# A new order of projections, a scheduler that prices dependent steps, and a second staging tile for values

## The chip, the cores and the metric

The kernel runs on one core of a Trainium2 chip. The metric is device time in microseconds; lower is better. The time before is a median of three runs, 1429.63 us (1425.99 to 1433.2).

## The reference, cut to what matters

One layer over 2048 frames of width 1024, with three groups of heads side by side, all in float32:

```python
u = x @ w_in
(fq, fk, fv, ff, fz, mq, mk, mv, mi, mf, mo, mz, rq, rz) = jnp.split(u, split_points, axis=-1)
y_fox = forgetting_attention(fq, fk, fv, ff + fox_f_bias) * jax.nn.silu(fz)
qk = jax.nn.silu(causal_depthwise_conv(jnp.concatenate([mq, mk], axis=-1), conv_w, conv_b))
mq_c, mk_c = jnp.split(qk, [MLSTM_WIDTH], axis=-1)
y_ml = mlstm(mq_c, mk_c, mv, mi + i_bias, mf + f_bias, mo, norm_g) * jax.nn.silu(mz)
mem_k, mem_v = jnp.split(mem @ w_mem_kv, [MEM_WIDTH], axis=-1)
y_mem = memory_attention(rq, mem_k, mem_v) * jax.nn.silu(rz)
y = jnp.concatenate([y_fox, y_ml, y_mem], axis=-1) @ w_out
return layer_norm(DEEPNORM_ALPHA * x + y, ln_g, ln_b)
```

`forgetting_attention` is causal softmax attention with 6 heads of 64, whose logits carry `c[query] - c[key]`, with `c` the running sum of the log forget gates. `mlstm` is a recurrent matrix memory with 4 heads of 96, computed in chunks; each chunk needs the state that the chunk before left. `memory_attention` is softmax attention of 4 heads of 64 into 256 memory tokens. A convolution over four frames and a SiLU stand before the mLSTM's queries and keys.

## The kernel before, in words

Every float32 operand of a large product is split into a high and a low part, and a product is three matmuls (high x high, low x high, high x low). The sequence is cut into four blocks of 512 frames, in two halves (`hf` 0 and 1, `bi` 0 and 1 within a half).

The kernel's work is written as small threads (Python generators). Each yields the next engine operation or asks for tiles. `Machine` (from line 131) is a list scheduler that runs while the program is built: it keeps a clock for each engine, gives each operation a price (`Op`, lines 91 to 112) and a time at which its inputs are there (`Machine.when`), and issues the ready operation with the lowest priority number on the engine that can start first. The times are a model's. What it fixes is the order of instructions on each engine; on the chip each engine takes its instructions in that order and waits where an input or a buffer isn't there.

- Projections (`projections`, one thread) run in the order of the list `SEQ`, one string for each half. An entry is a kind and a number, for both blocks or, with `.0` or `.1`, for one: `gate` (the gate logits and the attention's values), `mk mk mv` (memory keys and values), `rq` (memory queries, two heads each), `h` (queries and keys of one attention head), `y` and `z` (SiLU gates), `r` (the mLSTM's rows: values, output gate, gate), `c` (the mLSTM's queries and keys; each block gets a convolution of three multiply-add taps on VectorE, tile `cv`). One entry for one block is 24 matmuls of 512 columns, or 4 x 24 of 384 or 398 for `r` and `gate`. They go to PSUM tiles `pj`.
- Weights come by a loader: a DMA into `raw`, the high part `h` by ScalarE, the low part `l` by VectorE. High and low of a piece take one tile each of the tag `w`, together.
- In a `gate` job each of four row tiles is followed by `post`: the gate logits are added to `g14`, the values are split into high and low in a staging tile `vs` (ScalarE, then VectorE), and a DMA writes it to the scratch tensor `v_all`. When all eight tiles of a half are through, `gates` runs: log-sigmoid steps on VectorE up to the tiles `lsp`, which TensorE transposes, then cumulative sums (`tensor_tensor_scan`) on VectorE.
- Attention is a queue of 40 items (one head, one block; 0 to 7 and 20 to 27 are memory attention). For each, `att_max` (scores with queries in rows, tile `mx`, maxima on VectorE), `att_qk` and `att_exp` (scores `st`, two exponentials on ScalarE into `ph` and `p`, the low part `pl` on VectorE, the sum of `p` into `acc` on GpSimd) and `att_pv` (product `o` with the values) work in chunks of 128 keys; items run one after another in each. Items 32 to 35 are heads 2 and 3 of the second half, 36 to 39 heads 4 and 5. An item of block 2 has 12 chunks, one of block 3 has 16.
- The 16 mLSTM units (`ml_unit`, 128 frames each) start when all weights of the projections have been asked for and the last attention item is queued. Units are chains of short steps on all engines, and tile by tile they depend on the state.
- The output stage (`out_tile`) does the last product, for 16 tiles of 128 frames, once the mLSTM and all attention of a block are there.

`BUFS` gives the number of buffers of each tag; a thread that finds none waits.

Of the kernel before, what the change touches and what calls it, by code (L numbers as in the profile page):

```python
# [73 lines left out]
class Op:  # L74


    def __init__(self, eng, fn, args, kw):
# [8 lines left out]
        cols = size(out)  # L86
# [4 lines left out]
        if eng == "PE":  # L91
            f32 = ins[0].dtype == F32
            if f32 and fn.__name__ != "transpose":
                self.cost = 2.0 * max(2.0 * cols / 2.4, 107.0)
            else:
                self.cost = max((2.0 if f32 else 1.0) * cols / 2.4 + 14.0, 110.0)
        elif eng == "ACT":
            self.cost = 70.0 + 0.835 * wide + 115.0 * sum(hasattr(kw.get(a), "tensor") for a in ("bias", "scale"))
        elif eng == "DVE":
            one = fn.__name__ in ("tensor_scalar", "tensor_copy")  # L100
            columns = sum(size(a) == 1 for a in ins)
            self.cost = 69.0 + (0.521 if one else 1.042) * wide + 60.0 * columns
        elif eng == "POOL":
            if kw.get("op") == ALU.pow:
                self.cost = 290.0 + 170.0 * cols
            else:
                self.cost = 120.0 + (2.15 if fn.__name__ == "tensor_tensor" else 0.95) * wide
        else:
            self.cost = 475.0
            self.nbytes = 4 * math.prod(out.shape)  # L110
            self.far = 800.0 if kw["in_"].tensor.space == "DRAM" else 0.0
# [13 lines left out]
        self.key = (prio, seq)  # L125


LAT = 200.0
DMA_NS, DMA_BPNS = (600.0, 750.0), 366.0


class Machine:
# [54 lines left out]
    def when(self, op):  # L187
        eng, w = op.eng, 0.0
        for nm in op.ins + [op.out]:
            t, by = self.wr.get(nm, (0.0, eng))  # L190
            if by != eng or eng == "SP":
                w = max(w, t + LAT)
        return max(w, self.rd.get(op.out, 0.0))

    def issue(self, op):
# [70 lines left out]
class Engine:  # L266
# [5 lines left out]
    def __getattr__(self, fn):  # L272
# [1 line left out]
        return lambda *args, **kw: Op(self.name, f, args, kw)  # L274


BUFS = dict(x=32, raw=2, w=19, kb=6, qb=4, v=9, p=2, ph=2, pl=3, acc=1, zs=4, tz=2, vs=1, y=2, ta=4, sm=11, sc=2,
            rr=2, gs=4, g14=1, lsp=2, st=2, mx=2, pj=3, o=1)
PSUM_TAGS = ("st", "mx", "pj", "o")
RAW = ("raw", "p")  # L280
# [5 lines left out]
FAST = 8  # L286
LEAD = (1, 2)

SEQ = ("gate0 mk0.0 mk1.0 mv2.0 rq0 r0 y0 rq1 h0 y1 h1 r1 z0 h2 h3 r2 z1 c0 h4 c2 h5 c1 z2 c3.0 c4.0 c5.0 c3.1 c4.1 c5.1",
       "gate0 rq1 y1 rq0 y0 h0 r0 h1 z0 h2 r1 h3 z1 h4 c1 c2 c0.0 h5 z2 c0.1 r2 c4 c3.0 c5.1 c5.0 c3.1")  # L290


def _order():
# [1119 lines left out]
```

## Time and profile before

| what | value |
|---|---|
| median of the three runs | 1429.63 us |
| the profiled execution | 1436.65 us, span 1434.9 us |
| mean granted TensorE clock | 0.971 |
| TensorE busy (matmuls) | 1337.3 us, 93% |
| VectorE busy | 1057.1 us, 74% |
| ScalarE busy | 651.1 us, 45% |
| GpSimd busy | 486.5 us, 34% |
| DMA, mean over the span | 117 GB/s |

All instructions come from one helper, so all carry line 209, and groups are told apart by the names of their tiles: `out<-in`. PE is TensorE, DVE VectorE, ACT ScalarE, POOL GpSimd. A row of a window gives its ends, its length, the busy us of PE, PE's weight loads, DVE, ACT and POOL with their counts, the clock granted to TensorE, the busy share of the DMA engines and GB/s. A row of waits gives the total, the number of waits and the longest.

### The profile page before, as it was taken

The numbers are of one execution on the slowest core, as the hardware profiler recorded it, in microseconds if no ns is written. First come the engines' busy times: TensorE is split into PE (matmuls) and PEld (weight loads), VectorE is DVE, ScalarE is ACT, GpSimd is POOL, SyncE is SP. The second block draws the span as 40 slices with busy tenths as digits, with TensorE's granted clock in tenths as the row PEclk, the third lists the DMA queues.
The fourth block names the chain that finished last, engine by engine and source line by source line (L and its number), as shares of the span: only waits on it lengthen the run. The fifth ranks groups of instructions, "written<-read, shape, count | busy, mean of one in ns | idle before, by whom it ended". The sixth has DMA issues, their size and how long they took to land.

```text
span 1434.9 us, 20374 instructions
## 1 busy us (share of the span) xinstructions
PE 1337.3 (93%) x6648; PEld 1116.6 (78%) x6648; DVE 1057.1 (74%) x2082; ACT 651.1 (45%) x1371; POOL 486.5 (34%) x430
## 2 busy tenths in 40 slices
PE   7799999999999999899999998988999859999998
PEld 7778778888877897678887876656887648778886
DVE  4684687567578866879788878977888887668455
ACT  4423454335344542354536455453536676465100
POOL 3001233305103300025626456362544544355300
PEclk9999999999999999999999999999999969999999
DMA  6612421440531354141330431104012479775552
GB/s 205 224 46 78 136 74 62 128 127 23 171 110 54 114 177 144 51 142 57 100 97 18 135 107 49 50 30 126 33 44 92 128 211 281 218 211 176 195 164 85
DMA packets 136666, 167.54 MB, mean 117 GB/s; under 512 B 13760, under 2 KB 90832, under 8 KB 136560
## 3 DMA queue, kind: packets, MB, share of 16 engines
q1 hardware_dynamic: 136560, 166.24, 37.6%
q8 instruction: 53, 0.87, 0.3%
q14 instruction: 53, 0.43, 0.1%
HBM read 107.05 MB, written 50.29 MB: 110 GB/s over the span
## 4 chain that ended last, share of the span: by engine, by line
PE 62%; DVE 16%; DMA 9%; ACT 5%; issue 4%; POOL 3%; SPq 1%; DVEq 0%; ACTq 0%; POOLq 0%
PE pj L209 45%; PE st L209 6%; PE o L209 6%; PE mx L209 5%; DVE pl L209 3%; DMA v_all<-vs 3%; POOL acc L209 2%; DVE cv L209 2%; DMA dd<-m_scr 2%; DVE l L209 2%; DMA raw<-in_wg_dram 1%; DVE mp L209 1%; DVE mx L209 1%; DVE r L209 1%; ACT h L209 1%
## 5 line engine op out<-in xcount | busy, mean ns | idle before, releaser
L209 POOL TENSOR_TENSOR acc<-acc,p 128x512 f32<-128x512 f32 (+2 forms) x232 | 319.9, 1379 | 468.6 <-ACT p L209 174.1
L209 PE MATMUL pj<-h,h 128*128 128x512 f32 (+3 forms) x1144 | 428.0, 374 | 13.7 <-ACT h L209 8.8
L209 PE MATMUL pj<-l,h 128*128 128x512 f32 (+3 forms) x1144 | 421.1, 368 | 0.3 <-DVE l L209 0.2
L209 PE MATMUL pj<-h,l 128*128 128x512 f32 (+3 forms) x1144 | 421.0, 368 | 0.3
L209 PEld LDWEIGHTS pj<-h,h 128*128 128x128 f32 x1144 | 218.5, 191 | 41.0 <-ACT h L209 9.8
L209 PEld LDWEIGHTS pj<-l,h 128*128 128x128 f32 x1144 | 218.1, 191 | 27.8 <-DVE l L209 1.2
L209 PEld LDWEIGHTS pj<-h,l 128*128 128x128 f32 x1144 | 217.2, 190 | 27.5 <-DVE l L209 1.7
L209 DVE TENSOR_TENSOR pl<-p,ph 128x512 fp32r<-128x512 f32 (+2 forms) x185 | 190.8, 1038 | 29.6 <-ACT p L209 23.3
L209 ACT ACTIVATE ph<-st 128x512 fp32r<-128x512 f32 (+2 forms) x218 | 120.0, 555 | 101.1 <-PE st L209 88.4
L209 DVE TENSOR_TENSOR l<-raw,h 128x512 fp32r<-128x512 f32 (+2 forms) x194 | 137.7, 736 | 36.9 <-ACT h L209 35.4
L209 ACT ACTIVATE p<-st 128x512 f32<-128x512 f32 (+2 forms) x232 | 125.3, 546 | 46.6 <-POOL acc L209 27.3
L209 ACT CAST h<-raw 128x512 fp32r<-128x512 f32 (+2 forms) x194 | 108.3, 585 | 74.3 <-DMA raw<-in_wg_dram 40.8
L209 PE MATMUL o<-pl,v 128*128 128x512 f32 (+2 forms) x272 | 106.8, 396 | 13.6 <-DVE pl L209 13.1
L209 PE MATMUL st<-qm,km 68*128 68x512 f32 (+2 forms) x272 | 105.0, 386 | 11.5 <-ACT p L209 8.7
L209 PE MATMUL st<-qb,kb 128*128 128x512 f32 (+2 forms) x272 | 110.0, 404 | 0.0
L209 DVE TENSOR_REDUCE mp<-mx 128x1 f32<-128x512 f32 x144 | 95.3, 684 | 15.6 <-PE mx L209 14.7
L209 PE MATMUL pj<-h,yh 128*128 128x512 f32 (+1 forms) x264 | 106.2, 402 | 0.0
L209 PE MATMUL mx<-km,qm 66*128 66x512 f32 (+2 forms) x304 | 99.4, 366 | 7.2 <-DVE mp L209 2.8
L209 PE MATMUL pj<-h,ylo 128*128 128x512 f32 (+1 forms) x264 | 102.6, 389 | 0.0
L209 PE MATMUL pj<-l,yh 128*128 128x512 f32 (+1 forms) x264 | 102.1, 387 | 0.0
L209 PE MATMUL o<-ph,v 128*128 128x512 f32 (+2 forms) x218 | 84.0, 386 | 0.0
L209 POOL TENSOR_TENSOR y<-y,zs 128x512 f32<-128x512 f32 x20 | 30.2, 1512 | 146.4 <-DVE y L209 89.5
(184 smaller groups left out, 1929.4 us busy)
## 6 DMA issues: line engine op xcount, KB each, us to landing
raw<-in_wg_dram SPq DMA_DIRECT2D x76, 256.0 KB
raw<-in_wg_dram SPq DMA_DIRECT2D x48, 192.0 KB
v<-v_all SPq DMA_DIRECT2D x36, 256.0 KB
raw<-in_xt_dram SPq DMA_DIRECT2D x32, 256.0 KB
xr<-in_x_dram SPq DMA_DIRECT2D x32, 256.0 KB
out_dram<-xr SPq DMA_DIRECT2D x32, 256.0 KB
v_all<-vs SPq DMA_DIRECT2D x16, 384.0 KB
row_scr<-stg SPq DMA_DIRECT2D x32, 192.0 KB
```

Source lines behind the costliest of these rows:

```text
L209: op.fn(*op.args, **op.kw)
```

## The change

The scheduler's model: a scan on VectorE costs 60 + 2.3 ns a column (before, as any operation there, 69 + 1.042); the latency from one engine to another is taken as 300 ns (before 200); and an operation that reads what the same engine wrote waits 118 ns (not on TensorE). The smallest price of a four-pass float32 matmul goes from 107 to 112. Buffers: `vs` 1 to 2, `w` 19 to 18. `SEQ`: both strings are new. Each instruction does what it did; how many of each there are stays the same.

```diff
             if f32 and fn.__name__ != "transpose":
-                self.cost = 2.0 * max(2.0 * cols / 2.4, 107.0)
+                self.cost = 2.0 * max(2.0 * cols / 2.4, 112.0)
...
+        elif fn.__name__ == "tensor_tensor_scan":
+            self.cost = 60.0 + 2.3 * wide
         elif eng == "DVE":
...
-LAT = 200.0
+LAT, OWN = 300.0, 118.0
...
             if by != eng or eng == "SP":
                 w = max(w, t + LAT)
+            elif eng != "PE" and nm in op.ins:
+                w = max(w, t + OWN)
...
-BUFS = dict(x=32, raw=2, w=19, kb=6, qb=4, v=9, p=2, ph=2, pl=3, acc=1, zs=4, tz=2, vs=1, y=2, ta=4, sm=11, sc=2,
+BUFS = dict(x=32, raw=2, w=18, kb=6, qb=4, v=9, p=2, ph=2, pl=3, acc=1, zs=4, tz=2, vs=2, y=2, ta=4, sm=11, sc=2,
...
-SEQ = ("gate0 mk0.0 mk1.0 mv2.0 rq0 r0 y0 rq1 h0 y1 h1 r1 z0 h2 h3 r2 z1 c0 h4 c2 h5 c1 z2 c3.0 c4.0 c5.0 c3.1 c4.1 c5.1",
-       "gate0 rq1 y1 rq0 y0 h0 r0 h1 z0 h2 r1 h3 z1 h4 c1 c2 c0.0 h5 z2 c0.1 r2 c4 c3.0 c5.1 c5.0 c3.1")
+SEQ = ("gate0 mk0.0 mk1.0 mv2.0 rq0 r0 y0 y1 rq1 h0 h1 z0 r1 h2 c0 h3 z1 h4 h5 r2 c2 c3.0 z2 c1 c4.0 c5.0 c3.1 c4.1 c5.1",
+       "rq0 gate0 rq1 y1 y0 h0 h1 r0 z0 h2 r1 z1 h3 h4 r2 c1 c0.0 c2 z2 c4 h5 c5.0 c0.1 c3.0 c3.1 c5.1")
```

The order of instructions moves on every engine. Three places on TensorE follow. The first is where the transposes of the first `lsp` stand, behind the first gate job. Before, the memory values (256 columns) are done and a `rq` projection (512 columns) has begun:

```order
L209 MATMUL pj_732<-h_648,h_477 128x256
L209 MATMUL pj_732<-l_649,h_477 128x256
L209 MATMUL pj_732<-h_648,l_478 128x256
L209 MATMUL pj_832<-h_189,h_659 128x512
L209 MATMUL pj_832<-l_190,h_659 128x512
L209 MATMUL pj_832<-h_189,l_660 128x512
L209 MATMUL pj_858<-ident_r,lsp_818 6x128 x4
```

The same place now:

```order
L214 MATMUL pj_728<-h_609,h_456 128x256
L214 MATMUL pj_728<-l_610,h_456 128x256
L214 MATMUL pj_728<-h_609,l_457 128x256
L214 MATMUL pj_796<-ident_r,lsp_721 6x128 x4
L214 MATMUL pj_728<-h_609,h_456 128x256
```

The transposes have moved to the front by 24 matmuls, 21 of the memory values among them.

The second place is item 35 (head 3, block 3), in its middle. `qb` and `kb` are the low parts of its queries and keys, `v` its values. Before:

```order
L209 MATMUL st_9933<-qm_110,km_105 128x512
L209 MATMUL st_9933<-qb_9303,kb_8767 128x512
L209 MATMUL o_9820<-pl_9932,v_8490 128x512
L209 MATMUL o_9820<-ph_9928,v_8502 128x512
L209 MATMUL st_9946<-qm_110,km_106 128x512
L209 MATMUL st_9946<-qb_9303,kb_9266 128x512
L209 MATMUL o_9820<-pl_9945,v_8502 128x512
```

The same item now, with matmuls of the row projection `r2` (384 columns) between the chunks:

```order
L214 MATMUL st_9873<-qm_110,km_106 128x512
L214 MATMUL st_9873<-qb_9303,kb_9266 128x512
L214 MATMUL pj_9810<-h_9337,h_5477 128x384
L214 MATMUL pj_9810<-l_9338,h_5477 128x384
L214 MATMUL pj_9810<-h_9337,l_5478 128x384
L214 MATMUL o_9754<-pl_9872,v_8492 128x512
L214 MATMUL o_9754<-ph_9868,v_8492 128x512
L214 MATMUL mx_9882<-rb_111,sel 128x512
```

What stood as attention alone (51 rows without a projection) now has projections in it. The projections `c1 c2 c0`, which stood beside items 34 and 35, come behind them.

The third place is the end of the projections. Before, item 39's chunks stand between the last ones:

```order
L209 MATMUL st_11635<-qm_108,km_102 128x512
L209 MATMUL st_11635<-qb_10895,kb_10850 128x512
L209 MATMUL pj_11641<-h_5425,h_11157 128x512
L209 MATMUL pj_11641<-l_5426,h_11157 128x512
L209 MATMUL pj_11641<-h_5425,l_11158 128x512
L209 MATMUL o_11479<-pl_11634,v_9060 128x512
```

Now item 38's chunks stand behind the last projection matmul, with the score matmuls (`mx`) of item 39's maxima between them:

```order
L214 MATMUL mx_11515<-km_102,qm_108 128x512
L214 MATMUL st_11513<-qm_110,km_107 128x512
L214 MATMUL st_11513<-qb_10880,kb_11079 128x512
L214 MATMUL o_11452<-pl_11491,v_10106 128x512
L214 MATMUL mx_11525<-km_102,qm_108 128x512
L214 MATMUL o_11452<-ph_11503,v_10112 128x512
```

All of items 38 and 39, 28 chunks, and the first mLSTM units now come after the projections; before, 7 chunks did.

## Prediction

> **What bounds the kernel now.** I read the page's first two parts first, then windows of 50 us, to see where TensorE's time goes.
>
> ```profile
> span 1434.9 us, 20374 instructions
> ...
> PE 1337.3 (93%) x6648; PEld 1116.6 (78%) x6648; DVE 1057.1 (74%) x2082; ACT 651.1 (45%) x1371; POOL 486.5 (34%) x430
> ...
> PEclk9999999999999999999999999999999969999999
> ...
> 1150.00:1200.00 50.00, 35.85 (x215) 31.66 (x216) 40.46 (x115) 34.91 (x98) 22.37 (x21) 0.75 0.78 227
> 1350.00:1400.00 50.00, 50.00 (x226) 41.15 (x225) 28.90 (x52) 1.72 (x4) 3.62 (x5) 1.00 0.56 179
> ```
>
> TensorE (PE) is busy 1337.3 of 1434.9 us, and the change takes no matmul away. What can move is the idle 97.6 us and the stretches at a lower granted clock (the column after POOL's). The output stage (second window row) has neither. So I look for the places where PE stands still, and at what it waits for. First the waits of PE from 0 to 130 us, and ScalarE's (ACT's) copies into the staging tile `vs` from the timeline, the last of the first gate job and the last two of the second; a bracket is idle time and what ended it.
>
> ```profile
> PE pj L209 <- DVE lsp L209: 4.6, 1, 4.6
> PE pj L209 <- DVE vs L209: 3.2, 3, 1.6
> ...
> 59.93 0.48 ACT L209 CAST vs<-pj 128x384 fp32r<-128x384 f32 x1 [0.41 <-DMA v_all<-vs]
> 545.20 0.48 ACT L209 CAST vs<-pj 128x384 fp32r<-128x384 f32 x1 [3.31 <-DMA v_all<-vs]
> 552.20 0.48 ACT L209 CAST vs<-pj 128x384 fp32r<-128x384 f32 x1 [1.22 <-DMA v_all<-vs]
> ...
> 49.60 0.34 PE L209 MATMUL pj<-h,l 128*128 128x398 f32 x1
> 544.38 0.34 PE L209 MATMUL pj<-h,l 128*128 128x398 f32 x1
> ```
>
> One `vs` tile makes each copy wait until the DMA of the one before has landed. The last two rows are the last matmuls of the two gate jobs: the copies of their results start 10.0 us (59.93) and 7.5 us (552.20) behind them, and the gate arithmetic comes after that. Windows of 4 us there, and of 5 us behind the first gate job:
>
> ```profile
> 560.00:564.00 4.00, 1.52 (x9) 1.15 (x9) 3.70 (x15) 0.00 (x0) 0.00 (x0) 1.00 0.00 0
> 564.00:568.00 4.00, 3.32 (x9) 2.77 (x10) 3.90 (x9) 0.00 (x0) 0.00 (x0) 0.50 0.02 6
> 568.00:572.00 4.00, 4.00 (x18) 2.91 (x16) 2.21 (x6) 0.60 (x1) 0.52 (x1) 0.65 0.02 4
> 588.00:592.00 4.00, 1.12 (x6) 0.69 (x5) 3.81 (x10) 0.20 (x1) 0.00 (x0) 0.91 0.10 25
> 592.00:596.00 4.00, 3.95 (x13) 3.20 (x13) 1.97 (x4) 0.58 (x1) 0.00 (x0) 0.50 0.07 13
> 596.00:600.00 4.00, 4.00 (x21) 3.36 (x20) 3.38 (x10) 3.27 (x7) 0.00 (x0) 0.74 0.34 99
> ...
> 65.00:70.00 5.00, 0.99 (x5) 0.78 (x6) 4.34 (x18) 0.23 (x1) 0.00 (x0) 0.91 0.72 214
> 70.00:75.00 5.00, 5.00 (x19) 3.98 (x18) 4.45 (x9) 1.79 (x5) 0.00 (x0) 0.75 0.29 107
> ```
>
> A stall is paid twice: 2.48 us idle in the window at 560, then two windows at 0.50 and 0.65 of the clock.
>
> The other losses are in the second half of the attention and where the projections end: windows around item 35 (head 3, block 3, no projection matmul in its middle), the longest waits of PE between 1138 and 1190 us, the last projection matmul and the first output product.
>
> ```profile
> 910.00:938.00 28.00, 24.89 (x109) 18.52 (x107) 27.38 (x45) 15.93 (x33) 13.83 (x9) 1.00 0.11 34
> 938.00:972.00 34.00, 27.74 (x111) 19.48 (x110) 25.79 (x31) 19.50 (x37) 23.25 (x16) 0.92 0.08 32
> ...
> PE pj L209 <- DMA mk<-qk_scr: 5.6, 1, 5.6
> PE pj L209 <- ACT cv L209: 5.4, 2, 4.1
> PE st L209 <- ACT p L209: 4.7, 1, 4.7
> ...
> 1138.54 0.39 PE L209 MATMUL pj<-h,l 128*128 128x512 f32 x1
> 1189.51 0.40 PE L209 MATMUL pj<-h,yh 128*128 128x512 f32 x1
> ```
>
> From the last projection to the first output product pass 51.0 us, with the three waits above, 15.7 us, and some 5 us of shorter ones: the mLSTM units' chains of small steps have no projections beside them.
>
> **Part by part.** The model's new prices put no instruction in or out; they and the new list only change order. The 19th `w` tile goes: weights are taken in pairs (hi, lo), so 19 tiles made nine pairs and 18 do too. It could serve the late stage as one of many spares; I cost it at nothing, at most 2 us if the first output tiles wait for it.
>
> A, the first gate job (`vs` 1 to 2, transposes at another place). It can remove the two rows above, 4.6 + 3.2 us, and the slow clock behind them (0.99 x 0.09 + 5 x 0.25 = 1.3 us): at most 9. The gate arithmetic takes this long once the last copy is through (VectorE's, DVE's, timeline; first and last step):
>
> ```profile
> 61.56 0.18 DVE L209 TENSOR_SCALAR nx<-g 128x80 f32<-128x80 f32 x1
> 69.12 0.17 DVE L209 COPY lsp<-g 128x16 f32<-128x16 f32 x1
> ```
>
> That is 7.7 us. If the last copy comes at about 50 to 51 instead of 59.93 (its matmul ends 49.9), `lsp` is ready near 58-59. PE stood before the transposes from about 64.4 (69.0 less 4.6); it comes 3.2 us earlier without the `vs` waits, and about 3 more, since 21 short matmuls of the memory values and 3 of the next projection no longer stand ahead of them: near 58. So most goes, not all: **-7** (-9 to -1). DVE is the next limit behind it.
>
> B, the second gate job. The first episode costs 2.48 + 0.68 idle and 3.32 x 0.50 + 4 x 0.35 at the slow clock, 6.2 us; the second, where PE waits for DVE's rows, 2.88 + 0.10 + 3.95 x 0.50 + 4 x 0.26 = 6.0. In the new order two memory-attention projections go ahead of the gate job, and the attention of their four heads stands between its matmuls, where DVE has room: at 528-544 it has little to do.
>
> ```profile
> 528.00:532.00 4.00, 4.00 (x24) 4.00 (x23) 0.67 (x2) 0.48 (x1) 0.00 (x0) 1.00 0.34 138
> 540.00:544.00 4.00, 4.00 (x24) 4.00 (x23) 0.73 (x2) 0.48 (x1) 0.00 (x0) 1.00 0.18 69
> ```
>
> The first episode should go, since the last copy can come some 6 us earlier (-6); of the second a third (-2). Against that, the four heads' DVE work (a head has four `pl` of 0.68 to 1.12 and some six steps like the 0.684 reduction, rows below: about 8 us, 32 in all) meets some 25 us of free DVE time in 33 us of gate matmuls (192, at 23 or 24 in 4 us; four fifths of it free by the two windows); part of the 7 us left over can stall PE: +2. Sum **-6** (-12 to +5).
>
> C, items 32 to 37. Before, three convolution projections (`c1 c2 c0`) stand beside items 34 and 35, and each block of one puts three taps on DVE. In the new order a row projection (`r2`) takes their place, and the convolutions move behind item 35. Means by form:
>
> ```profile
> L209 DVE TENSOR_TENSOR pl<-p,ph 128x512 fp32r<-128x512 f32 x130 | 144.6, 1117 | 25.3 <-ACT p L209 21.6
> L209 DVE TENSOR_REDUCE mp<-mx 128x1 f32<-128x512 f32 x144 | 95.3, 684 | 15.6 <-PE mx L209 14.7
> L209 DVE SCALAR_TENSOR_TENSOR cv<-u,cw_sb,cv 128x512 f32<-128x512 f32 x72 | 60.1, 834 | 6.6 <-ACT cv L209 4.8
> L209 DVE TENSOR_TENSOR l<-raw,h 128x512 fp32r<-128x512 f32 x130 | 96.8, 767 | 31.1 <-ACT h L209 30.4
> ```
>
> The window 910-938 has DVE at 27.4 of 28 us and PE idle 3.1; 938-972 has PE idle 6.3 us, and 34 x 0.08 = 2.7 of slow clock. That is 12.1 us to win; the convolutions' taps crowd DVE again behind item 35, where no exponentials run: +3. **-9** (-14 to 0).
>
> D, the end of the projections. Head 5 (`h5`) moves behind `z2 c4`, so items 38 and 39 with their 28 chunks now come after the last projection matmul instead of 7. By the order's columns about 103 full matmuls move from before that point to after it. Their spacing is this:
>
> ```profile
> 1371.60 22.00 PE pj L209 x96
> ```
>
> 22.00 / 96 = 0.229 us, so 103 x 0.229 = 23.6 us, and the stretch of before with the same PE work is 23.6 + 51.0 = 74.6 us. Between the first mLSTM product and the first output product the new order has, on DVE, 6 more `pl` (6.7 us), 17 more reductions (at most 11.6), 3 more products of the units (2) and 10 taps and 3 `l` less (8.3 + 2.3): about +9 us on an engine that is near its limit there. On PE there are some 14 matmuls less: -3. The attention can fill the 21 us of waits, which speaks for less than +9; but without projections chunks come densely, and DVE's `pl` then runs at this pace:
>
> ```profile
> 862.88 0.68 DVE L209 TENSOR_TENSOR pl<-acc,ph 128x512 fp32r<-128x512 f32 x1
> 867.34 16.20 DVE L209 TENSOR_TENSOR pl<-p,ph 128x512 fp32r<-128x512 f32 x10
> 863.70 20.43 POOL L209 TENSOR_TENSOR acc<-acc,p 128x512 f32<-128x512 f32 x13 [5.86 <-ACT ta L209]
> ```
>
> 1.62 us each beside GpSimd's adds (20.43 / 13 = 1.57), 0.68 without them. At that pace 28 of them cost 28 x (1.62 - 1.117) = 14 us more: upper end +23, lower -3. I take **+8**, near the count.
>
> The Trainium skill's page "SBUF — State Buffer", section "SBUF: two separate sides", speaks against this part: it holds the port pair of VectorE and GpSimd to be an exclusive lock, the later instruction being fully blocked. By that, one chunk would take 0.68 plus an add's whole length, 2.25 us, and D would be 18 us dearer; the rows above (1.62) do not bear that out.
>
> Elsewhere (130-518, 600-850, from 1190) the same work is permuted with PE as the bound; I take 0, give or take 5. Sum: -7 - 6 - 9 + 8 = -14 us. The profiled execution took 1436.65 us (1.75 around its span), which makes 1422.6; it lies 7.0 above the median of the runs shown, 1429.63, so against that median I forecast **1416 us**.
>
> **The rivals.**
> - The tail eats the gain. The units' chains stay as serial as before and the attention adds to them: 51.0 - 7 x 1.62 = 39.7 us of chains, 28 x 1.62 = 45.4 of chunks, 16 reductions of 0.684 = 10.9 between them: 96 us for 74.6, D = +21. With A to C at -22 this gives 1429, no change. For it: PE takes its instructions in order, so a unit's product that waits holds up the chunks behind it. Against it: ACT and DVE work on chunks while PE waits.
> - Slower. The same tail falls to the half clock that the windows show behind every stall. Four matmuls of a chunk then take 4 x 0.458 = 1.83 us, over 1.62: 39.7 + 28 x 1.83 + 10.9 + 16 x 0.458 = 109 us, D = +35, 1443 us. It decides against the change once the tail is over 74.6 + 22 + 7 = 104 us. For it: PE's share there would be near 57% (4 x 0.229 of 1.62), and the window at 560 with 38% was followed by 0.50. Against it: the window 938-972, with the same pace and PE at 82%, kept 0.92 on the mean. The Trainium skill's "TensorE: Matmul & The Clock Gate", section "HAM oscillation", has PE throttle after idle stretches over about 3.4 us; gaps between chunks are shorter, so by that rule this rival would be less likely.
> - The second `vs` tile brings nothing: DVE's or the DMA queue's pace ends the gate wait in its place (A -1, B 0), -1 - 9 + 8 = -2, 1428 us. For it, DVE is busy 4.34 of 5 us at 65-70.
>
> **How the numbers follow.** Forecast 0.58, tail eats the gain 0.18, slower 0.16, the tile brings nothing 0.08. A measurement here tells about 0.5%, 7.1 us, so faster is below 1422.5 and slower above 1436.8: faster 0.58, same 0.26, slower 0.16. The forecast's own range is 1398 to 1430 (C at its best and D at +3, or B and C near their worse ends). The range for all, 1398 to 1440, leaves out 1 in 10 below and, of the slower case, about the same above.
>
> **What would show it.** ACT's `vs` copies no longer wait 3 us for `v_all`, the last one stands within 2 us of its gate job's last matmul, and the `lsp` wait is under 2 us: A and B right. Windows around item 35 with PE over 95% busy and DVE under 80%: C right. The time from the last projection matmul to the first output product: near 83 us at D = +8; over 104 the slower rival holds. The forecast is wrong if PE's idle time is not some 10 us less, or if it grows in the stretches that I took as unchanged.

## The result and the profile after

The changed kernel takes 1380.82 us in the median (1378.44 to 1383.99 in four runs), the kernel before 1429.58 us beside it. The ratio is 0.966, with a 95% interval of 0.9627 to 0.9694: 48.8 us faster. The forecast was 1416 us, with a range from 1398 to 1430; the measurement lies below it. The sign was right, and the gain is more than three times the one forecast. One execution of one experiment (the own wait alone) ran at a granted clock of 0.741 and took 1631.99 us, and is left out everywhere.

The first lines of the page of after:

```profile
span 1382.3 us, 20376 instructions
...
PE 1322.7 (96%) x6648; PEld 1110.4 (80%) x6648; DVE 1045.8 (76%) x2082; ACT 653.5 (47%) x1371; POOL 489.1 (35%) x430
...
PEclk9999999999999999999999999999999879999999
```

PE does the same 6648 matmuls and now stands idle for 1382.3 - 1322.7 = 59.6 us instead of 97.6. The matmuls themselves take 14.6 us less, at a higher clock (0.983 on the mean, before 0.971): the prediction's windows showed the clock at 0.50 behind stalls, and with a stall its slow clock goes too.

The same moment in two different orders finds different work being done, so the two traces can't be set side by side moment by moment; at the same amount of work done they can. So I count TensorE's matmul columns as each kernel issues them, in units of one 512-column matmul ("position"), and take from the trace the time at which the matmul at a position starts. Six stretches cover the program: 0-400 the first gate job, 400-2000 the first half's projections and attention, 2000-2600 the second gate job, 2600-3300, 3300-4100 the items 32 to 37, 4100-4800 the end of the projections with the mLSTM units. What follows is the end of the output stage. (Not every short matmul of the mLSTM units is in this count: counted one by one from the trace, the last mark lies at some 4851 to 4854 full matmuls, which shifts a difference between two kernels by less than 1 us.) The windows between these positions, before and then after, with the first two stretches in one row:

```profile
0.00:518.00 518.00, 490.50 (x2468) 417.42 (x2469) 356.26 (x718) 230.41 (x452) 124.75 (x140) 0.99 0.37 115
518.00:681.00 163.00, 152.17 (x736) 128.13 (x735) 121.49 (x268) 63.45 (x122) 31.10 (x27) 0.96 0.32 103
681.00:854.00 173.00, 168.74 (x827) 141.57 (x826) 141.19 (x209) 86.75 (x171) 86.45 (x65) 1.00 0.31 95
854.00:1078.00 224.00, 206.50 (x922) 159.65 (x921) 188.36 (x285) 109.64 (x210) 105.28 (x74) 0.98 0.18 55
1078.00:1334.00 256.00, 225.55 (x1261) 191.82 (x1260) 198.07 (x511) 156.24 (x409) 125.86 (x112) 0.92 0.65 190
```

```profile
0.00:500.00 500.00, 481.52 (x2451) 413.86 (x2452) 351.10 (x712) 228.22 (x446) 122.53 (x138) 0.99 0.37 117
500.00:660.00 160.00, 153.53 (x749) 129.77 (x748) 124.48 (x269) 65.02 (x126) 29.27 (x26) 0.98 0.39 119
660.00:830.00 170.00, 167.71 (x836) 142.57 (x835) 142.35 (x217) 89.23 (x176) 89.66 (x68) 1.00 0.26 79
830.00:1030.00 200.00, 195.09 (x907) 157.65 (x906) 172.38 (x259) 110.31 (x206) 98.98 (x67) 1.00 0.24 76
1030.00:1281.00 251.00, 230.64 (x1271) 188.48 (x1271) 201.85 (x524) 154.69 (x407) 135.57 (x118) 0.94 0.63 187
```

The largest change is in the fourth row: items 32 to 37 took 224 us with PE idle for 17.5, and take 200 with PE idle for 4.9. The steps that the prediction named, in the trace of after, first the last `vs` copies and the last matmuls of their gate jobs:

```profile
50.71 0.48 ACT L214 CAST vs<-pj 128x384 fp32r<-128x384 f32 x1 [3.81 <-DVE g L214]
557.26 0.48 ACT L214 CAST vs<-pj 128x384 fp32r<-128x384 f32 x1 [4.07 <-DVE g L214]
...
50.08 0.34 PE L214 MATMUL pj<-h,l 128*128 128x398 f32 x1
556.64 0.34 PE L214 MATMUL pj<-h,l 128*128 128x398 f32 x1
```

Each copy now starts 0.3 us behind the end of its last matmul, where it started 10.0 and 7.5 us behind. Then the windows at item 35 (the first of the three) and behind it:

```profile
910.00:934.00 24.00, 23.58 (x122) 20.45 (x122) 19.76 (x20) 15.72 (x31) 22.53 (x16) 1.00 0.13 48
934.00:958.00 24.00, 23.97 (x111) 19.05 (x110) 22.57 (x42) 13.01 (x23) 1.92 (x2) 1.00 0.72 223
958.00:981.00 23.00, 23.00 (x103) 18.78 (x102) 22.28 (x46) 11.43 (x20) 4.12 (x3) 1.00 0.31 105
```

PE is 98% busy at item 35 and DVE 82% (19.76 of 24 us). Behind it, where the convolutions went, DVE is 97% busy (22.28 of 23 us) and PE doesn't stand still at all: the crowd that I priced at 3 us is there and costs PE nothing in this window. Last, the tail from the last projection to the first output product:

```profile
1064.61 0.39 PE L214 MATMUL pj<-h,l 128*128 128x512 f32 x1
1145.98 0.47 PE L214 MATMUL pj<-h,yh 128*128 128x512 f32 x1
```

That is 81.4 us; the forecast was 83, the slower rival began at 104.

### The profile page after: what moved, and what is told of

The parts are those of the page before. It is cut to its first block, busy times and chain, and to the rows that moved or that the text cites. A ratio compares the mean times of both kernels' runs of the same rounds, so it can differ in the third digit from the quotient of the medians.

```text
span 1382.3 us, 20376 instructions
## 1 busy us (share of the span) xinstructions
PE 1322.7 (96%) x6648; PEld 1110.4 (80%) x6648; DVE 1045.8 (76%) x2082; ACT 653.5 (47%) x1371; POOL 489.1 (35%) x430
## 4 chain that ended last, share of the span: by engine, by line
PE 69%; DVE 15%; DMA 5%; issue 3%; POOL 3%; ACT 3%; SPq 1%; DVEq 0%; ACTq 0%; POOLq 0%
PE pj L214 52%; PE st L214 6%; PE o L214 6%; PE mx L214 5%; DVE pl L214 3%; POOL acc L214 2%; DVE mp L214 1%; DVE l L214 1%; DMA raw<-in_wg_dram 1%; DVE cv L214 1%; SPq L214 1%; DVE mx L214 1%; DVE r L214 1%; DVE sc L214 1%; DVE qb L214 1%
## 5 line engine op out<-in xcount | busy, mean ns | idle before, releaser
L214 DVE TENSOR_TENSOR pl<-p,ph 128x512 fp32r<-128x512 f32 (+2 forms) x189 | 196.2, 1046 | 20.4 <-ACT p L214 16.7
L214 DVE TENSOR_TENSOR l<-raw,h 128x512 fp32r<-128x512 f32 (+2 forms) x194 | 129.2, 692 | 42.1 <-ACT h L214 37.5
L214 PE MATMUL st<-qb,kb 128*128 128x512 f32 (+2 forms) x272 | 110.9, 408 | 0.0
## 6 DMA issues: line engine op xcount, KB each, us to landing
raw<-in_wg_dram SPq DMA_DIRECT2D x76, 256.0 KB
v<-v_all SPq DMA_DIRECT2D x36, 256.0 KB
raw<-in_xt_dram SPq DMA_DIRECT2D x32, 256.0 KB
xr<-in_x_dram SPq DMA_DIRECT2D x32, 256.0 KB
out_dram<-xr SPq DMA_DIRECT2D x32, 256.0 KB
```

What stands on the lines that cost most here:

```text
L214: op.fn(*op.args, **op.kw)
```

## The experiments

All runs stand in one table: the median, the ratio to the kernel before as it was measured beside that run (medians from 1429.19 to 1431.69 us) with its interval, then the time of each stretch in the run's profile. Medians of different rows were partly taken on different chips, so a difference of a few us between two rows is safer by the ratios. Profiles of one order differ by 2 to 4 us in a stretch: to position 400 three experiments below (taps, r2 first, 18 weight tiles) keep the order of before and took 120.9, 118.9 and 118.6 us, so the 122.5 of before holds some 3 us of chance.

| kernel | us | ratio (95%) | 0-400 | 400-2000 | 2000-2600 | 2600-3300 | 3300-4100 | 4100-4800 |
|---|---|---|---|---|---|---|---|---|
| before | 1429.58 | | 122.5 | 389.5 | 163.0 | 172.6 | 223.4 | 256.0 |
| after | 1380.82 | 0.966 (0.9627-0.9694) | 110.9 | 385.0 | 156.1 | 170.7 | 200.3 | 251.2 |
| before, new buffers | 1437.32 | 1.0039 (1.0018-1.006) | 119.3 | 390.8 | 157.4 | 171.7 | 222.5 | 268.1 |
| before, new prices | 1399.51 | 0.9791 (0.9765-0.9817) | 113.5 | 381.3 | 147.0 | 171.8 | 220.5 | 253.4 |
| before, first list | 1427.78 | 0.998 (0.9961-0.9998) | 119.3 | 389.5 | 159.6 | 173.2 | 221.2 | 255.1 |
| before, second list | 1407.62 | 0.9855 (0.9823-0.9888) | 121.3 | 387.6 | 165.2 | 170.4 | 202.6 | 255.7 |
| after, old prices | 1406.28 | 0.9827 (0.9806-0.9848) | 118.7 | 388.6 | 161.8 | 170.5 | 202.6 | 253.8 |
| after, old buffers | 1386.11 | 0.9685 (0.9667-0.9702) | 113.8 | 386.6 | 155.9 | 170.0 | 200.8 | 249.7 |
| before, short taps | 1424.44 | 0.9962 (0.9944-0.998) | 120.9 | 388.6 | 160.2 | 172.7 | 218.5 | 253.6 |
| before, r2 first | 1430.04 | 0.9999 (0.9983-1.0014) | 118.9 | 389.9 | 161.6 | 173.3 | 209.5 | 270.3 |
| before, short adds | 1401.19 | 0.9785 (0.9754-0.9816) | 120.2 | 384.8 | 157.7 | 166.9 | 210.4 | 253.0 |
| before, w 18 | 1445.39 | 1.0089 (1.0062-1.0115) | 118.6 | 390.4 | 161.7 | 172.6 | 225.7 | 266.8 |
| before, own wait | 1418.53 | 0.9904 (0.9872-0.9935) | 119.2 | 391.4 | 150.7 | 172.9 | 218.9 | 253.3 |
| before, latency 300 | 1429.71 | 0.9989 (0.9971-1.0007) | 118.3 | 390.3 | 155.6 | 172.9 | 227.7 | 254.8 |
| before, scan price | 1430.72 | 1.0019 (0.9995-1.0043) | 118.8 | 390.1 | 159.4 | 174.5 | 225.7 | 253.4 |
| before, own wait + latency | 1411.65 | 0.9891 (0.9856-0.9925) | 115.4 | 382.5 | 157.8 | 173.0 | 224.4 | 246.7 |
| after, own wait 0 | 1398.26 | 0.9807 (0.9759-0.9856) | 116.6 | 387.7 | 152.1 | 169.1 | 200.0 | 260.1 |
| after, short adds | 1359.44 | 0.9513 (0.9482-0.9544) | 108.0 | 380.3 | 154.9 | 167.4 | 193.7 | 244.4 |
| after, old first list | 1379.59 | 0.9643 (0.9615-0.967) | 111.6 | 379.6 | 155.1 | 170.7 | 200.3 | 247.7 |
| after, old first list and buffers | 1384.27 | 0.9675 (0.9651-0.9699) | 113.8 | 379.8 | 155.7 | 171.1 | 201.1 | 250.3 |

### The four parts, each alone in the kernel before

Buffers:

```diff
-BUFS = dict(x=32, raw=2, w=19, ... vs=1,
+BUFS = dict(x=32, raw=2, w=18, ... vs=2,
```

> The kernel before with the buffers alone (vs 2, w 18); prices and list as before. Theory 1 (each gain sits at its own place: gate stalls by the tile, items 32 to 37 by the second list): both gate stalls go, A at its -12 and the first episode of B at -6, nothing else moves: about -16 us. Theory 2 (the prices make the order, the rest only follows): the transposes still stand where the old prices put them, -5 us or less.

Prices (the two new rules, the latency and the minimum, as in the change's diff, nothing else):

> The kernel before with the new prices alone (latency 300, own 118, scans, 112). Theory 1: the order shifts by a few instructions, within 5 us of before. Theory 2: most of the gain, -25 us or more, items 32 to 37 and the mLSTM units behind the first output product among it.

The first string of `SEQ` alone, and the second alone:

> The kernel before with the new list of the first half alone. Theory 1: what positions between the gate jobs gained, -4 us, and nothing else: -2 to -6. Theory 2: no gain, within 3 us or slower, since the old prices place the items.

> The kernel before with the new list of the second half alone. Theory 1: the gain of items 32 to 37 (-23), the tail at +7, half of B: -15 to -22 us, with PE over 95% busy around item 35. Theory 2: less than -10, since the old prices put chunks and projections beside one another as badly as before.

Two parts carry the gain: the prices alone 30 us (0.9791) and the second list alone 21 to 24 (0.9855; 1431.14 - 1407.62 = 23.5). The first list alone is worth 0.2%, and the buffers alone cost 0.4%. The prices of the model were the part that I had put at nothing. The second list brings its gain at items 32 to 37 (202.6 us there, alone and with all the rest but the prices), the prices bring most of theirs ahead of them, up to position 2600.

### The parts taken out of the kernel after

Old prices with the new lists and buffers (the change's first three hunks undone), and the old buffers with the new lists and prices:

```diff
-BUFS = dict(x=32, raw=2, w=18, ... vs=2,
+BUFS = dict(x=32, raw=2, w=19, ... vs=1,
```

> The changed kernel with the old prices (latency 200, no own wait, scans as any operation). Theory 1 (parts add): it loses the 31 us that the prices gave by themselves: about 1412 us. Theory 2 (the new lists were good only under the new prices): worse than the new second list alone, over 1416.

> The changed kernel with the old buffers (vs 1, w 19). Theory 1 (parts add; the buffers alone made it 6 us slower): 1375 to 1381 us, so the second staging tile is not needed. Theory 2 (the tile pays once the transposes come at the right place): the copies wait for the DMA again and both gate jobs stall, 1388 us or more.

Without the new prices the gain at the first gate job is gone (118.7 where the order of before has 118.6 to 122.5), and so is nearly all of it at the second (161.8). Without the second `vs` tile most of both stays (113.8 and 155.9), and the time is 5 us over the kernel after. So most of what I had credited to the staging tile is the prices' doing. PE's waits say how. Below, waits of the whole run, of the kernel before and then of the new prices on the old lists with the first lines of its page:

```profile
PE mx L209 <- DVE r L209: 10.6, 16, 2.9
...
PE pj L209 <- DVE lsp L209: 6.7, 2, 4.6
...
PE mx L209 <- DVE rr L209: 3.5, 2, 2.2
PE pj L209 <- DVE vs L209: 3.2, 3, 1.6
...
PE mx L209 <- DVE m L209: 1.9, 2, 1.4
```

```profile
span 1395.2 us, 20363 instructions
...
PE 1316.9 (94%) x6648; PEld 1107.0 (79%) x6648; DVE 1048.5 (75%) x2082; ACT 653.3 (47%) x1371; POOL 488.6 (35%) x430
...
PE pj L213 <- DVE lsp L213: 3.8, 1, 3.8
...
PE pj L213 <- DVE vs L213: 3.0, 3, 1.3
...
PE mx L213 <- DVE r L213: 1.7, 2, 1.0
```

`m`, `r` and `rr` are the last steps of an item's maxima: VectorE reduces, scales and subtracts, TensorE transposes, VectorE copies. Like the steps to `lsp` they are chains in which each step reads the one before. PE's waits for these four tiles come to 22.7 us before and 5.5 with the new prices; the `vs` wait stays at 3.0 and the first `lsp` wait at 3.8 (4.6 before), and still 30 us are gone. Between the two profiled executions PE's idle time falls by 19.3 us (78.3 for 97.6), not much more than what these four waits lost, 17.2; its busy time falls by 20.4 us, at a clock of 0.982 on the mean for 0.971. One place of before shows what the old prices missed (DVE, timeline, then PE):

```profile
585.01 1.36 DVE L209 TENSOR_TENSOR_SCAN lf<-qrow 4x128 f32<-4x128 f32 x4
...
586.77 0.67 DVE L209 TENSOR_TENSOR lf<-lf,mc 4x512 f32<-4x512 f32 x1
587.48 0.68 DVE L209 TENSOR_TENSOR qrow<-mc,lf 4x512 f32<-4x512 f32 x1
...
590.83 0.67 DVE L209 TENSOR_REDUCE m<-mx 128x2 f32<-128x512 f32 x1
591.53 0.17 DVE L209 TENSOR_SCALAR r<-m 128x4 fp32r<-128x4 f32 x1
591.74 0.16 DVE L209 SCALAR_TENSOR_TENSOR r<-m,r 128x4 fp32r<-128x4 f32 x1
591.82 0.68 DVE L209 TENSOR_TENSOR pl<-p,ph 128x512 fp32r<-128x512 f32 x1
592.42 0.69 DVE L209 TENSOR_REDUCE m<-mx 128x2 f32<-128x512 f32 x1
```

```profile
592.05 0.27 PE L209 MATMUL mx<-ident_r,r 128*8 128x128 f32 x1 [2.92 <-DVE r L209]
592.11 0.73 PE L209 MATMUL pj<-h,h 128*128 128x512 f32 x1
```

The `pl` at 591.82 has nothing to do with the reduction behind it: that starts 0.60 us later, before the `pl` has ended. The step at 587.48 reads the `lf` of the one before, of the same width, and starts 0.71 us behind it; the `r` at 591.53 reads the `m` of the one before and starts 0.70 behind. The old price, 69 + 1.042 x 512 = 603 ns, is right for the first kind; with the own wait of 118 ns it is right for the second, 721. Over the whole trace of before, neighbours among the single rows of DVE's timeline without a wait between them fall into two kinds: 280 in which the second reads the tile that the first wrote have 0.03 us between end and start in the median; the 696 others start 0.08 us before the end. That is 0.11 us a step. The scheduler thought such chains shorter than they are, set the transposes of `r` too early in PE's row, and PE, which takes its row in order, stood 2.92 us and then ran matmuls at 0.50 of the clock (a `pj` of 0.73 us at 592.11).

Not all of these 2.92 us is the prices' doing. Ahead of the rows above, the last of four scans took 1.44 us and the other three some 0.39 each, with an add of GpSimd beside it, which ended 0.28 us before the scan did:

```profile
581.76 2.40 DVE L209 TENSOR_TENSOR_SCAN br<-ones_c,lf 4x128 f32<-4x128 f32 x4
...
582.42 1.46 POOL L209 TENSOR_TENSOR acc<-acc,p 128x512 f32<-128x512 f32 x1 [13.39 <-ACT p L209]
```

With the adds shortened in the same order (an experiment below), that scan takes 0.47 us and the longest wait for `r` at the second gate job is 1.8 us. So about 1.1 us of the wait is this contention, and the rest is left for the prices.

### The prices one by one

The own wait alone, the latency alone, the scan price alone, and own wait with latency, in the kernel before; then the kernel after with an own wait of 0:

```diff
-LAT = 200.0
+LAT, OWN = 200.0, 118.0
...
+            elif eng != "PE" and nm in op.ins:
+                w = max(w, t + OWN)
```

> The kernel before with the own wait of 118 ns alone. Theory O (chains of dependent steps on one engine, the gate's and the mLSTM's, were priced too short): most of the prices' 31 us, -20 or more, at the gate jobs and where the projections end. Theory L (the latency between engines): -8 or less.

```diff
-LAT = 200.0
+LAT = 300.0
```

> The kernel before with the latency between engines at 300 instead of 200 alone. Theory L: most of the prices' 31 us, -20 or more, spread over all the attention (fewer waits of products for pl, exponentials and reductions). Theory O: -8 or less.

```diff
+        elif fn.__name__ == "tensor_tensor_scan":
+            self.cost = 60.0 + 2.3 * wide
```

> The kernel before with the scan's price alone. Theory S (the scans behind the gate jobs, 1.26 us each and priced at 0.60, put TensorE's transposes ahead of time): 10 us or more faster, at positions 0 to 400 and 2000 to 2600. Theory C (own wait and latency work only together): within 4 us of before.

> The kernel before with the own wait and the latency, without the scan's price. Theory S: about the sum of the two, -15 us. Theory C: close to all three prices, -26 or more.

```diff
-LAT, OWN = 300.0, 118.0
+LAT, OWN = 300.0, 0.0
```

> The changed kernel without the own wait (0), latency 300 and scans as changed. If the own wait carries the gain in the new order too: 1390 us or more, with waits of TensorE for lsp, r or rr back at the gate jobs. If the other prices stand in for it: within 4 us of the changed kernel.

PE's waits for `r`, `rr`, `lsp` and `m` follow the own wait more than anything else:

| kernel | the four waits, us | time, us |
|---|---|---|
| before | 22.7 | 1429.58 |
| scan price | 17.2 | 1430.72 |
| latency 300 | 17.5 | 1429.71 |
| own wait | 9.7 | 1418.53 |
| own wait + latency | 6.5 | 1411.65 |
| all prices | 5.5 | 1399.51 |
| after, old prices | 10.8 | 1406.28 |
| after, own wait 0 | 7.3 | 1398.26 |
| after | 4.0 | 1380.82 |

Latency and scan price do nothing measurable alone; the own wait gives 1%, and taking it out of the kernel after costs 17 us (1.5% by the ratios). There the four waits account for 3.3 us; by the stretches 5.7 us of the loss lie at the first gate job and 8.9 at the end of the projections (260.1 for 251.2), where I did not trace the waits. Together the prices give more than the sum: with own wait and latency the second gate job takes 157.8 us, with all prices 147.0. That is 11 of the 14.6 us between these two profiled executions. Two prices differ between them, the scan's and the raised minimum of a small matmul (107 to 112), and no run has the minimum alone. Besides, PE stands 5.0 us in the longer of the two for which its profile names no releaser, and 2.8 for `r`. So how much of the 11 us is the scan price's is not shown. The four scans of 128 columns in the fence above (`lf<-qrow`, 1.36 us in all) were priced at 69 + 1.042 x 128 = 202 ns each and take 340; the new price is 60 + 2.3 x 128 = 354. What the runs don't settle either is why the prices must come together; a row in which one chain is priced rightly and its neighbour is not may put the wait elsewhere, but that was only argued.

### Items 32 to 37: what the projections beside them do

Three theories of the idle PE there: the taps crowd DVE; the exponentials and the low parts (`pl`) go at the pace of GpSimd's adds, whatever stands beside; a chunk without projection matmuls is too little for PE. First the taps, in the order of before:

```diff
-            yield DVE.scalar_tensor_tensor(v_[:, 0:512], u[:, i:i + 512], cw_sb[:, j, i:i + 1], v_[:, 0:512],
+            tap = DVE.scalar_tensor_tensor(v_[:, 0:64], u[:, i:i + 64], cw_sb[:, j, i:i + 1], v_[:, 0:64],
...
+            tap.cost = 69.0 + 1.042 * 512 + 60.0
+            yield tap
```

> The kernel before in its own order, word for word, with the convolution taps over 64 of 512 columns (it leaves out the other 448), priced as before: only VectorE's time for them falls, by some 0.7 us of 0.834 each. Theory T (the taps beside items 34 and 35 hold up the low parts of the exponentials): positions 3300 to 3900 lose most of what the new list gained there, -15 us or more, item 35 among it. Theory F (item 35 has no projections between its chunks and runs at the pace of the adds): 3500 to 3700 stays within 4 us, item 35's stretch keeps its 34 us; 3400 to 3600 may gain 3.

The stretch goes from 223.4 to 218.5, against 200.3 in the kernel after: the taps are a small part at most. Then the entry `r2` alone, set ahead of `c1 c2 c0.0` in the old second list:

```diff
-       "gate0 ... z1 h4 c1 c2 c0.0 h5 z2 c0.1 r2 c4 c3.0 c5.1 c5.0 c3.1")
+       "gate0 ... z1 h4 r2 c1 c2 c0.0 h5 z2 c0.1 c4 c3.0 c5.1 c5.0 c3.1")
```

> The kernel before with one entry moved: r2 of the second half from behind c0.1 to ahead of c1. Theory F and T both: items 34 and 35 get r2 beside them and the convolutions come later; positions 3300 to 4100 take about 205 us instead of 223, -18. If the gain there needs the other moves of the list too: -8 or less.

This one move takes 14 us out of the stretch (209.5), and the end of the projections gives all 14 back (270.3 for 256.0). The gain is real at items 32 to 37, and it needs the rest of the list to be kept. Then the adds, in the order of before and in that of after:

```diff
-            yield POOL.tensor_tensor(acc[:, q0:BLK], acc[:, q0:BLK], p_[:, 0:nq], op=ALU.add)
+            add = POOL.tensor_tensor(acc[:, q0:q0 + 64], acc[:, q0:q0 + 64], p_[:, 0:64], op=ALU.add)
+            add.cost = 120.0 + 2.15 * nq
+            yield add
```

> The kernel before in its own order, word for word, with GpSimd's adds of the exponentials over 64 of 512 columns (it leaves out the rest of the row sums), priced as before. Theory F (chunks without projections go at the pace of the adds and of the low parts that these slow): item 35's stretch, positions 3600 to 3700, falls from 34 to 28 us or less, and pl from 1.1 to 0.7 us. Rival T2 (ScalarE's two exponentials or TensorE's slow clock set that pace): 32 us or more stay. In all 10 to 20 us faster by F, under 5 by T2.

> The changed kernel in its own order, with GpSimd's adds over 64 of 512 columns (it leaves out the rest of the row sums), priced as before; the old order gained 30 us by the same edit. If the new order had won the adds' price by putting projections between the chunks: 15 us or less, nearly all in the tail without projections, positions 4200 to 4400. If the adds hold up the low parts everywhere as much as before: 25 us or more, with items 32 to 35 among it.

The costliest forms with the adds shortened, in the order of before (GpSimd's add, DVE's `pl`), and `pl` in the kernel after as it is:

```profile
L209 POOL TENSOR_TENSOR acc<-acc,p 128x64 f32<-128x64 f32 x232 | 136.8, 592 | 596.9 <-ACT p L209 261.3 <-DVE pl L209 144.1 <-PE mx L209 89.7
...
L209 DVE TENSOR_TENSOR pl<-p,ph 128x512 fp32r<-128x512 f32 x130 | 93.2, 721 | 58.3 <-ACT p L209 57.8
```

```profile
L214 DVE TENSOR_TENSOR pl<-p,ph 128x512 fp32r<-128x512 f32 x126 | 140.1, 1115 | 15.8 <-ACT p L214 12.6
```

A `pl` takes 721 ns beside short adds and 1117 beside whole ones, in the new order as in the old (1115): the change leaves this contention where it was. Without it the old order gains 30 us, 13 of them at items 32 to 37, and the new one 21, with 6.6 there. Item 35's own stretch (positions 3600 to 3700) shows the shares: 34.4 us before, 29.9 with short adds, where the second theory expected 28 or less, and 24.3 with `r2` first. So the second theory holds for a part of the pace of the chunks, and the third has the larger part: with `r2` between the chunks PE has work while they go at their pace. What sets that pace beside the adds is not shown. What the contention is can be read from single rows of the trace of before:

```profile
865.38 1.30 POOL L209 TENSOR_TENSOR acc<-acc,p 128x512 f32<-128x512 f32 x1
...
865.97 1.26 DVE L209 TENSOR_TENSOR pl<-p,ta 128x512 fp32r<-128x512 f32 x1 [1.81 <-ACT p L209]
```

The add ends at 866.68, the `pl` 0.55 us behind it. So do most: of the 92 full-width low parts of `p` that start while an add runs, 81 end 0.54 to 0.56 us after the add's end, and take from 0.82 to 1.80 us; the 24 with no GpSimd work beside them take 0.67 to 0.69. So the `pl` waits for the add, and the wait is a part of its recorded time; the mean of 1117 ns lies between the two kinds. The Trainium skill's page "SBUF — State Buffer", section "SBUF: two separate sides", calls the port pair that VectorE and GpSimd share an exclusive lock, for which the later instruction waits. The trace agrees (81 of 92).

### The 19th weight tile

```diff
-BUFS = dict(x=32, raw=2, w=19, ...
+BUFS = dict(x=32, raw=2, w=18, ...
```

> The kernel before with 18 w tiles instead of 19, nothing else. Theory W (the spare tile serves the late stage: the buffers alone lost their 10 us behind the first output product by it): 5 to 12 us slower, all of it at positions 4300 to 4800. Rival: within 3 us, and the second staging tile's reordering did the harm.

In the old order its loss costs 0.9%, 13 us, and nearly all of it between positions 4100 and 4800 (266.8 for 256.0). In the new order the stretch is as long with 19 tiles and one `vs` tile (249.7) as with 18 and two (251.2). That accounts for the loss with the new buffers alone: 268.1 there, against gains of at most 3 and 6 us at the gate jobs. The second `vs` tile with 19 `w` tiles was not tried. The `r2` entry had the same effect on this stretch: the late order of before was easily upset. Which waits each of them brings there differs: with 18 tiles PE waits once for 6.7 us for the high part `h` of a weight and stands 4.0 us for which the profile names no releaser, with `r2` first it waits 7.8 us for a unit's `dd` and 4.5 for a DMA. Why is open.

### What the first list and the staging tile add

The kernel after with the first string of before; then also with the old buffers:

```diff
-SEQ = ("gate0 ... r0 y0 y1 rq1 h0 h1 z0 r1 h2 c0 h3 z1 h4 h5 r2 c2 c3.0 z2 c1 c4.0 c5.0 c3.1 c4.1 c5.1",
+SEQ = ("gate0 ... r0 y0 rq1 h0 y1 h1 r1 z0 h2 h3 r2 z1 c0 h4 c2 h5 c1 z2 c3.0 c4.0 c5.0 c3.1 c4.1 c5.1",
```

> The kernel after with the first half's list of before; prices, buffers and the second half's list stay new. If the prices alone bring the gain of the first half, and the new first list brings nothing of its own, the stretches up to the second gate job cost what they cost with the new prices on the old order: 641.8 us where the kernel after takes 652.0, and the later stretches stay as they are in the kernel after: near 1371 us, 10 below it. If the new first list is a part of the gain (it fits the new prices and buffers), the time is above 1386 us, 5 or more over the kernel after. If the late stage is shaken by any move, as the old order's was, the stretch of the mLSTM units is 10 us longer or more and the time is not below that of the kernel after.

> The kernel after with the first half's list and the buffers (one staging tile, 19 weight tiles) of before; prices and the second half's list stay new. Up to the end of the first half's work the order is that of the new prices on the old list, so 0 to 2000 should take 494.8 us as there, whatever the second list does. If the second staging tile is worth 5 us in every order, near 1376 us; if it is worth something only with the new first list, near 1370 us or at most 2 us over the variant with the new buffers.

1379.59 us: the new first list adds nothing (the kernel after has 1380.82, the intervals lie over each other). It is no faster version either: I had expected some 10 us less, since the prices on the old lists pass the first 2600 positions in 641.8 us and the kernel after in 652.0. To position 2000 this came (491.2 for 495.9), but the second gate job kept 155.1 us where the prices alone have 147.0, because the second list stands there. With the old prices that list costs nothing clear at this place (165.2 and 161.8 in its two runs, 160.2 to 163.0 in four runs of the old order), with the new ones some 8 us. The old buffers cost 4.7 us here and 5.3 in the kernel after (4 by the ratios): the new buffers are worth about 5 us with the new prices, under either first list.

## Why the forecast was too small, point by point

By place, the terms and what they measured: A and B -13, measured -15 to -19; C -9, measured -23; D +8, measured +5; everything else 0, give or take 5, measured -16 (positions 400 to 2000 and 2600 to 3300 -6, behind the first output product -10). So the 35 us that the forecast lacks lie mostly in C (14) and in the places at which it put nothing (16). By cause it was wrong in one more step, the prices.

- **The cause that was put at nothing**: "The model's new prices put no instruction in or out; they and the new list only change order", and no term of the sum is theirs. The prices bring 30 us alone and about 25 in the finished kernel, and by the stretches more than half of these lie at the two gate jobs (7.8 and 5.7 of 22 us). There I had booked 13 us on the tile and on the order of the list, so that A and B came out near their sizes is luck. I read the waits as waits for a staging tile or for a projection, and not as the mark of a scheduler that takes a chain for shorter than it is. The rows were there: 16 waits for `r` of 10.6 us in all, of which the prediction reads only those up to 130 us and from 1138 to 1190, and the 0.11 us between dependent and independent neighbours.
- **A, the first gate job** (-7, 110.9 for about 119 to 122.5: -8 to -12): its waits went as said (no `lsp` wait is left), and the size is near. The cause was mostly not the tile: with the tile and old prices nothing is gained there (118.7); with the prices and one tile it takes 113.8, so the tile adds 3 us to the prices' 5 to 9. The limit behind `lsp` was named ("DVE is the next limit behind it"); the prices moved it.
- **B, the second gate job** (-6, measured -7): the size is right, by luck, as a difference of two larger ones that the forecast didn't have. The prices give 16 us there in the old order (147.0) and the new second list gives back some 8. Of those, 5.7 lie in its first hundred positions (28.6 us for 22.9), beside the memory heads' steps on DVE, which I had put at +2. From 502 to 512 us of the trace of after DVE is busy for 9.78 of the 10 us, and PE waits for low parts `l` of weights.
- **C, items 32 to 37** (-9, measured -23): the place was right, the size wrong. Of the two reasons given, the taps beside items 34 and 35 count for 5 us at most (218.5 for 223.4), and the row projection between the chunks for 14 (209.5) and more. The size was missed in two ways. I took 62 us of windows, 910 to 972, and found 12.1 us to win; the row 854 to 1078 shows 17.5 us of idle PE and 224 x 0.02 = 4.5 of slow clock, 22 in all, and nearly all of it was won. And the +3 for the crowded DVE behind item 35 was not paid: PE stood still nowhere in the window where DVE was at 97%.
- **D, the tail** (+8, measured +5): the time to the first output product is as forecast (81.4 for 83); ahead of the last projection matmul 2 us more went than counted (from position 4100 to it 61.0 us before and 35.4 after, 25.6 less for 23.6).
- **Elsewhere** ("Elsewhere (130-518, 600-850, from 1190) the same work is permuted with PE as the bound; I take 0, give or take 5"): PE was not the only bound from 1190 on. From the first output product to the last mark both kernels have the same columns to do, and it takes 144.1 us before and 134.4 after (the first fence): PE's idle time goes from 7.3 to 3.0 us, and the slow clock, 144.1 x 0.04 = 5.8 us before, is gone. That is why the stretch 4100 to 4800 got 5 us shorter and not 8 longer. The waits that shrank are for the units' steps among the output products: 6.0 us before, between 1190 and 1300 us (the second fence), and 2.7 in the same 110 us of after, from 1146 (the third). Why they shrank was not tested.

```profile
1189.50:1333.60 144.10, 136.82 (x806) 118.19 (x805) 102.44 (x328) 83.25 (x243) 72.43 (x71) 0.96 0.76 224
...
1146.00:1280.40 134.40, 131.43 (x792) 112.12 (x791) 99.23 (x312) 81.25 (x237) 72.81 (x71) 1.00 0.78 231
```

```profile
PE pj L209 <- ACT kr L209: 2.8, 2, 2.0
PE pj L209 <- ACT nd L209: 1.9, 1, 1.9
PE pj L209 <- DVE dd L209: 1.3, 2, 1.0
```

```profile
PE pj L214 <- ACT nd L214: 1.2, 1, 1.2
PE pj L214 <- ACT n L214: 1.0, 2, 0.6
PE pj L214 <- DVE xr L214: 0.5, 1, 0.5
```

  In all these runs the stretch 4100 to 4800 lay between 244 and 270 us.
- **The 19th tile** ("at most 2 us") was 13 us in the old order; in the new one, where it was only tried together with the staging tile, its stretch shows nothing of it (249.7 and 251.2).
- **The rivals**: the tail took 81.4 us, and not the 96 and 109 of the two rivals that made it longer; the clock in its windows was 0.87 and 0.81, over the half clock of the slower one (rows below). The argument against that rival, that gaps under 3.4 us do no harm to the clock, did not hold all the same: the wait that ended at 592.05 was 2.92 us long and the window behind it ran at 0.50. On D the prediction sets the exclusive lock aside, since by it a chunk would take 2.25 us and the rows show 1.62. That sum takes the add's recorded time for its work; but adds and low parts start while the other runs, so their recorded times hold waits and can't be added. The trace of before bears the lock out (81 of 92, above), and 1.62 us is the pace with it: the 18 us that the prediction names for the lock were not to come on top.

```profile
1056.00:1095.00 39.00, 32.34 (x147) 24.24 (x146) 36.04 (x72) 23.96 (x48) 18.65 (x12) 0.87 0.50 153
1095.00:1150.00 55.00, 45.31 (x235) 35.51 (x234) 45.93 (x119) 37.92 (x104) 35.73 (x28) 0.81 0.47 142
```

The rival that the tile brings nothing was close to the truth on the tile and wrong on the time. The signs came nearly all as said: the copies behind their matmuls, the `lsp` wait, PE at item 35 over 95%, 83 us for the tail; only DVE at item 35 was at 82% and not under 80. They were signs of the places, and none of them could tell whose doing a gain was.

## What to carry to other kernels

When a scheduler fixes the order, its prices are part of the kernel: take from a trace of before the start-to-start times of dependent and of independent neighbours on one engine, compare them with the model, and add up PE's waits for the last tile of every short chain, over the whole run. Where a list moves work beside a slow stretch, price the whole stretch (its idle time plus the time lost to the clock), not the window where it shows first. And try a move with the order behind it: a gain of 14 us at one place was given back whole in the next stretch.

## What the runs showed of the hardware

- A step on VectorE that reads the step before starts some 0.11 us later than one that doesn't (+0.03 against -0.08 us from the end recorded for the first, medians of 280 and 696 pairs in the trace of before).
- A `pl` of 128x512 takes 1117 ns on the mean with GpSimd's adds of 1567 ns beside it and 721 with adds of 64 columns: 0.40 us of contention each, some 51 us of VectorE time over 130 of them.
- A `pl` that starts while a GpSimd add runs ends 0.54 to 0.56 us after the add's end (81 of 92 in the trace of before), whatever the add has left to do; its recorded time, 0.82 to 1.80 us, holds the wait.
- A scan of 4x128 on VectorE took 1.44 us beside a GpSimd add of 1.46 us, 0.39 us without one, and 0.47 in the same order with short adds.
- PE was 100% busy for 23 us beside a VectorE that was 97% busy (958 to 981 us of the kernel after).
